# Norm factors kept in PSUM, split weights used for both segments, and two conditions normalised in one VectorE pass

## The chip, the cores and the metric

One core of a Trainium2 chip runs the whole program. The metric is the device time of one execution in microseconds (us). Engines: TensorE (PE in the rows) multiplies matrices and writes to PSUM; VectorE (DVE), ScalarE (ACT) and GpSimd (POOL) do elementwise work; SyncE (SP) issues most DMAs. Each engine runs its own instruction list in order and waits on semaphores for the others.

## The reference, cut to what matters

Two layers of a diffusion trunk run over 640 tokens: 128 context tokens, conditioned by `c_ctx`, and 512 latent tokens, conditioned by `cond`. Layer 0 mixes with a state-space scan and a Conformer convolution, layer 1 with a Fourier transform over grouped channels; a ConvFFN follows each:

```python
for i in range(DEPTH):
    sh1, sc1, gt1, sh2, sc2, gt2 = split(silu(cond) @ w_mod[i] + b_mod[i], 6)
    hm = rmsnorm(x, g_mix[i]) * (1 + sc1) + sh1
    out = mixer(hm)                 # layer 0 ends in "@ w_out", layer 1 in "@ fnet_w + b"
    x = x + gt1 * out
    hf = rmsnorm(x, g_ffn[i]) * (1 + sc2) + sh2
    x = x + gt2 * conv_ffn(hf, w_up, conv_w, w_down)
y = rmsnorm(x, norm_f)
```

So a norm over all 1024 channels stands between each product that ends a sub-layer and the next product. Shift, scale and gate differ between the two conditions.

## The kernel before, in words

Activations lie transposed: 1024 channels are 8 tiles `x[:, k, :]` of 128 partitions by 640 tokens. Every fp32 product is done in three passes, as high part times high part, low times high and high times low (xh·wh, xl·wh, xh·wl; L224 to L233). `weights` (L202) loads a raw weight tile with a DMA from SP; `split` (L210) makes wh by a cast on ScalarE (L218) and wl by a subtraction on GpSimd (L221). Three buffers of each stand in the pool `wp`, five of raw.

For the last part of a product before a norm, the tokens are cut in two segments (`by_segment`, L378): all 8 output tiles m of segment 0, then all 8 of segment 1. Each tile goes through `residual` (L356, VectorE, reading PSUM), a square on ScalarE (L320) and an addition on VectorE (L324). After the eighth tile `finish` (L326) sums over partitions with a matmul by ones (L331, rows named `acc<-ssq,ones` and `acc<-sqt,ones`), and `rstd` (L292) makes the factor `bc`, which is the same on all partitions: one activation (L296) and three VectorE instructions (L297 to L299). The loads and splits of all 8 weight tiles are made once for each segment.

While TensorE works on segment 1, `then` normalises segment 0: `norm_split` (L345) multiplies x by `bc` and the scale A on VectorE (L342, one instruction for each condition), adds the shift on ScalarE (L350, which writes xh) and takes the rest on VectorE (L351, xl). Tile k is emitted NLAG = 4 output tiles late. The next consumer also starts early: `first_up` (L410) holds three w_up tiles, `FIRST`, and multiplies segment 0 of them for k = 0 to 3 before the second `finish` and for k = 4 to 7 after it; `rest` does segment 1 and `mods_between` (L430), the products of the next conditioning vectors (L440, 32 matmul records).

There are four such places, which the text calls A to D:

- A: the last half of `@ w_out`, segments of 320 tokens (607.9 to 661 us); segment 0 holds both conditions (128 and 192 tokens).
- B: the end of the first ConvFFN, going into the Fourier mixer; segments of 384 and 256 tokens.
- C: the end of `@ fnet_w`, like A.
- D: the end of the second ConvFFN, going into the final norm; 384 and 256 tokens.

PSUM is, from A on, four accumulators of 128 x 1024 fp32, which `acc` (L146) takes from one pool in rotation; in A, B and C a `finish` takes one for its sum and frees it after `rstd`. During the scan (250 to 510 us) there are other pools. The order within each engine isn't written by hand: a scheduler chooses it from dependences, pools and its own costs, so it can move lines that the diff doesn't touch.

Of the kernel before, what the change touches and what calls it, by code (L numbers as in the profile page):

```python
# [15 lines left out]
P = 128  # L16
D = 1024
# [31 lines left out]
NLAG = 4  # L49
RAWB = 5  # L50
# [86 lines left out]
def _body(nc, tc, st, A, O, dbg):  # L137
# [8 lines left out]
    def acc():  # L146
        return pools["acc"].tile([P, 1024], F32, tag="acc", name="acc")
# [6 lines left out]
    def set_banks(accs, small):  # L154

        while open_:
            open_.pop().__exit__(None, None, None)
        pools.clear()
        for name, n in (("acc", accs), ("misc", small)):
            if n:  # L160
                open_.append(tc.tile_pool(name=f"{name}{accs}", bufs=n, space=PS))
                pools[name] = open_[-1].__enter__()
# [141 lines left out]
    class SumSq:  # L304
# [3 lines left out]
        def __init__(self, bc=None, apart=True):  # L308
            self.apart = apart
            self.a = sm.tile([P, T], F32, tag="ssq", name="ssq", bufs=1)  # L310
            self.last = {}
            self.bc = bc or sm.tile([P, T], F32, tag="yss", name="bc", bufs=1)
# [13 lines left out]
        def finish(self, s, o):  # L326

            ps = misc()[:, 0:size(s)]
# [3 lines left out]
            bc = self.bc[:, o:o + size(s)]  # L332
            rstd(ps, bc)
            return bc
# [10 lines left out]
    def norm_split(x, bc, a, sh, k, xh, xl, s, gap=0):  # L345
        t = temp("hmt")
        modulated(t, x, bc, a, k, s)
        for sub, o, j in pieces(s):
            to = (sub[0] + j * gap, *sub[1:])
            S.activation(tok(xh[:, k, :], to), tok(t, sub), AF.Identity, bias=sh[:, k, j:j + 1])  # L350
            V.scalar_tensor_tensor(tok(xl[:, k, :], to), in0=tok(t, sub), scalar=sh[:, k, j:j + 1],  # L351
                                   in1=tok(xh[:, k, :], to).bitcast(F32), op0=ADD, op1=SUB)

# [24 lines left out]
    def by_segment(src, k0, acts, x, gt, segs, then, early=None):  # L378


        ss = SumSq()
        bc = {}
        early = early or (lambda k: None)
        for i, s in enumerate(segs):
            def after(m, ps):
                residual(x, m, ps, gt, s)
                ss.add(x[:, m, :], m, s)
                if m == 0:
                    rsqrt_table(x[:, m, s[0]:s[0] + 1])
                if i and m >= NLAG:  # L390
                    then(bc[0], segs[0], m - NLAG)

            product(src, k0, acts, (s,), after)
            if i:
                for k in range(KD - NLAG):
                    early(k)
            bc[i] = ss.finish(s, i * size(segs[0]))
# [3 lines left out]
        for k in range(KD):  # L401
            then(bc[1], segs[1], k)

    def transition(src, k0, acts, x, after, gt, then, early):
# [3 lines left out]
        by_segment(src, k0 + n, acts[n:], x, gt, SEGS, then, early)  # L408
# [664 lines left out]
    def ffn(l, x, xh, xl, background, mods, rest, segs, then, early=None):  # L1073
# [4 lines left out]
        with tc.tile_pool(name=f"ff{l}", bufs=1) as fp:  # L1078
# [62 lines left out]
            by_segment(wdn, *pend, x, gt, segs, then, early)  # L1141
# [215 lines left out]
```

## Time and profile before

| | us |
|---|---|
| runs | 1727.39, 1727.5, 1730.4 (median 1727.5) |
| profiled execution | 1728.85 |
| its span | 1727.1 |
| PE busy | 1636.6 (95%) |
| DVE busy | 1358.5 (79%) |
| ACT busy | 698.2 (40%) |
| POOL busy | 804.9 (47%) |

Times in rows are microseconds from the start of the span. A row of a timeline is start, duration, engine, line, operation, output<-inputs, shape and count; a bracket gives the idle time of that engine just before it and who ended it. Matmul ends are modelled, so the distance between two starts (the pitch) says more than a duration. The granted clock of TensorE is given as a share of 2.4 GHz.

### The profile page before, as it was taken

What the parts mean: (1) busy time and instruction counts of PE and PEld (TensorE: products, weight loads), DVE (VectorE), ACT (ScalarE), POOL (GpSimd) and SP (SyncE); (2) the same over time, 40 slices, a digit from 0 to 9 for tenths busy, and PEclk for the clock granted to TensorE, in tenths of its full rate; (3) what the DMA queues carried; (4) which work ended last, traced back from release to release, by engine and by line L of the source; (5) the groups of instructions that cost most, each with busy time, mean ns of one, the idle gap of its engine ahead of it and who ended that gap; (6) DMA issues with size and microseconds to landing.
All of it is one profiled execution on the core that took longest, in us unless ns stands there. A gap on an engine that the chain in (4) does not pass through costs nothing.

```text
span 1727.1 us, 27861 instructions
## 1 busy us (share of the span) xinstructions
PE 1636.6 (95%) x10794; PEld 1570.9 (91%) x10794; DVE 1358.5 (79%) x2398; ACT 698.2 (40%) x1211; POOL 804.9 (47%) x526
## 2 busy tenths in 40 slices
PE   8898998999899989999999999889899999999997
PEld 5797988889799979999999999779799999999996
DVE  7788696978764788899999999864899848818846
ACT  4322236888853254322331232545633223313324
POOL 1342335655653444563555465404446545534544
PEclk9999999999999999999999999999999999999998
DMA  7455332332332443235224323402532222222123
GB/s 299 155 170 178 120 122 86 111 105 70 96 131 96 136 132 98 62 105 191 71 86 159 134 59 107 144 26 74 176 110 86 75 86 74 73 86 74 47 59 116
DMA packets 81911, 189.20 MB, mean 110 GB/s; under 512 B 7540, under 2 KB 33043, under 8 KB 81780
## 3 DMA queue, kind: packets, MB, share of 16 engines
q1 hardware_dynamic: 78980, 184.29, 33.8%
q10 hardware_dynamic: 2800, 3.15, 0.6%
q8 instruction: 85, 1.39, 0.3%
q14 instruction: 46, 0.38, 0.1%
HBM read 183.57 MB, written 3.83 MB: 109 GB/s over the span
## 4 chain that ended last, share of the span: by engine, by line
PE 43%; DVE 22%; issue 3%; ACT 2%; POOL 1%; DMA 0%; DVEq 0%; POOLq 0%; ACTq 0%
PE acc L229 40%; DVE cva L1104 8%; DVE mm L270 6%; DVE x L356 2%; DVE modc L274 1%; DVE cva L1093 1%; DVE ssq L324 1%; POOL wl L221 1%; PE acc L331 1%; PE acc L440 1%; ACT sqt L320 1%; DVE x L1261 1%; PE acc L1228 0%; DVE hmt L342 0%; ACT fh L1235 0%
## 5 line engine op out<-in xcount | busy, mean ns | idle before, releaser
L221 POOL TENSOR_TENSOR wl<-raw,wh 128x512 fp32r<-128x512 f32 (+5 forms) x314 | 561.6, 1797 | 660.8 <-ACT wh L218 658.2
L229 PE MATMUL acc<-xh,wh 128*128 128x320 f32 (+2 forms) x2064 | 490.1, 315 | 14.8 <-ACT wh L218 7.1
L229 PE MATMUL acc<-xh,wl 128*128 128x320 f32 (+2 forms) x2064 | 487.8, 313 | 6.8 <-POOL wl L221 6.8
L1104 DVE SCALAR_TENSOR_TENSOR cva<-acc,cw,cva 128x504 f32<-128x504 f32 (+2 forms) x704 | 479.2, 692 | 16.6
L229 PE MATMUL acc<-xl,wh 128*128 128x320 f32 (+2 forms) x2064 | 488.2, 313 | 0.2
L218 ACT CAST wh<-raw 128x512 fp32r<-128x512 f32 (+5 forms) x314 | 238.3, 769 | 573.9 <-PE acc L229 413.6
L229 PEld LDWEIGHTS acc<-xh,wh 128*128 128x128 f32 (+1 forms) x2064 | 352.1, 190 | 21.6 <-ACT wh L218 9.1
L229 PEld LDWEIGHTS acc<-xh,wl 128*128 128x128 f32 (+1 forms) x2064 | 351.5, 190 | 9.3 <-POOL wl L221 8.3
L229 PEld LDWEIGHTS acc<-xl,wh 128*128 128x128 f32 (+1 forms) x2064 | 351.9, 190 | 2.6 <-issue 0.9
L356 DVE SCALAR_TENSOR_TENSOR x<-acc,modc,x 128x128 f32<-128x128 f32 (+2 forms) x240 | 112.3, 498 | 126.8 <-PE acc L229 125.8
L229 PE MATMUL acc<-fh,wl 128*128 128x320 f32 (+2 forms) x832 | 206.7, 311 | 2.9 <-POOL wl L221 2.8
L229 PE MATMUL acc<-fh,wh 128*128 128x320 f32 (+2 forms) x832 | 206.6, 311 | 2.2 <-DVE x L356 2.2
L229 PE MATMUL acc<-fl,wh 128*128 128x320 f32 (+2 forms) x832 | 206.4, 310 | 0.0
L229 PEld LDWEIGHTS acc<-fh,wl 128*128 128x128 f32 x832 | 143.8, 189 | 4.6 <-POOL wl L221 4.3
L229 PEld LDWEIGHTS acc<-fh,wh 128*128 128x128 f32 x832 | 143.9, 189 | 2.9 <-issue 2.5
L229 PEld LDWEIGHTS acc<-fl,wh 128*128 128x128 f32 x832 | 143.6, 188 | 0.6
L270 DVE SCALAR_TENSOR_TENSOR mm<-mm 128x1024 f32<-128x1024 f32 x80 | 138.1, 1726 | 1.2 <-DMA mm<-in_w_modT 0.2
L1119 POOL TENSOR_TENSOR cva<-cva 128x640 f32<-128x640 f32 x44 | 72.2, 1641 | 87.8 <-ACT cva L1118 87.8
L270 DVE SCALAR_TENSOR_TENSOR mjunk<-mraw,crow 128x1024 f32<-128x1024 f32 x68 | 97.4, 1433 | 7.8 <-DMA mraw<-in_w_modT 7.4
L1093 DVE SCALAR_TENSOR_TENSOR cva<-acc,cw,cva 128x127 f32<-128x127 f32 x176 | 61.0, 346 | 49.3 <-ACT cva L1089 44.2
L1123 POOL TENSOR_TENSOR fl<-cva,fh 128x640 fp32r<-128x640 f32 x44 | 71.0, 1613 | 34.5 <-ACT fh L1122 34.5
L1118 ACT ACTIVATE cva<-cva 128x640 f32<-128x640 f32 x44 | 32.4, 737 | 119.9 <-DVE cva L1104 113.3
(248 smaller groups left out, 1896.8 us busy)
## 6 DMA issues: line engine op xcount, KB each, us to landing
raw<-in_ffn_w_up SPq DMA_DIRECT2D x88, 512.0 KB, 3.6
raw<-in_w_in SPq DMA_DIRECT2D x40, 512.0 KB, 3.7
mm<-in_w_modT SPq DMA_DIRECT2D x40, 512.0 KB, 3.6
mraw<-in_w_modT SPq DMA_DIRECT2D x34, 512.0 KB, 3.7
e<-acsd SPq DMA_DIRECT2D x40, 256.0 KB, 3.2
raw<-in_ffn_w_down SPq DMA_DIRECT2D x32, 256.0 KB, 2.6
raw<-in_ffn_w_down SPq DMA_DIRECT2D x16, 448.0 KB, 3.4
raw<-in_w_out SPq DMA_DIRECT2D x24, 256.0 KB, 3.2
```

Source lines behind the costliest of these rows:

```text
L218: S.copy(wh[:, ks, :], raw[:, ks, :])
L221: G.tensor_tensor(wl[:, ks, :], raw[:, ks, :], wh[:, ks, :].bitcast(F32), op=SUB)
L229: PE.matmul(part(ps, s), lhsT=wt[:, k, :], rhs=tok(at, s), start=(k == 0 and p == 0), stop=(k == n - 1 and p == 2))
L270: V.scalar_tensor_tensor(junk, in0=raw[:, cs_], scalar=1.0, in1=crow[j][:, cs_], op0=MULT, op1=MULT, accum_out=m[:, 2 * o + j:2 * o + j + 1])
L274: V.tensor_scalar(modc[l][:, i, :], m[:, 0:2], b, None, op0=ADD)
L320: S.activation(t, tok(x_ap, s), AF.Square)
L356: last = V.scalar_tensor_tensor(tok(x[:, m, :], sub), in0=part(ps, s, o, sub), scalar=gt[:, m, j:j + 1], in1=tok(x[:, m, :], sub), op0=MUL ...
L1093: V.scalar_tensor_tensor(a[:, lo:hi], in0=ps[:, BASE + lo + d:BASE + hi + d], scalar=w(1, c), in1=a[:, lo:hi], op0=MULT, op1=ADD)
L1104: last = V.scalar_tensor_tensor(av[:, r0:r1, c0:c1], in0=pv[:, r0 + dr_:r1 + dr_, c0 + dc:c1 + dc], scalar=w(r, c), in1=av[:, r0:r1, c0:c1 ...
L1118: S.activation(cv[1], cv[1], AF.Silu)
L1119: G.tensor_tensor(cv[0], cv[0], cv[1], op=MULT)
L1123: G.tensor_tensor(l_, cv[0], h_.bitcast(F32), op=SUB)
```

## The change

Three edits in the code of `by_segment` and its helpers:

1. `acc` turns explicitly over tags acc0 to acc3. `SumSq(held=True)` takes one accumulator out of that turn at the first `finish`; the sum and the factor `bc` of both segments stay in it (segment 0 from column 0, segment 1 from 512) until `by_segment` ends. `rstd` works in a scratch tile `t` and writes `bc` with its last instruction. This holds in A, B and C; D keeps `bc` in SBUF.
2. Weight tiles split for segment 0 are used again for segment 1. In A and C (`kept=4`) tiles 4 to 7 stay in a pool of their own and 1 to 3 in `wp`, so only tile 0 is loaded and split again, and segment 1 goes in the order 1, 2, 3, 0, 4, 5, 6, 7. In B and D (`kept=0`) the order is 5, 6, 7, 0 to 4 with three tiles used again. That is 20 DMAs, 20 casts and 20 subtractions fewer.
3. `norm_split` for a segment with two conditions (segment 0 of A and C): VectorE multiplies x by `bc` over 320 tokens at once; ScalarE applies scale and shift in place for each condition and copies to xh; VectorE subtracts over 320. Four VectorE and two ScalarE instructions become two and three, for each of 8 tiles.

```diff
+    def acc(hold=False):
+        i = turn["next"]
+        if i == turn["held"]:
+            i = (i + 1) % turn["n"]
+        turn["next"] = (i + 1) % turn["n"]
+        if hold:
+            turn["held"] = i
+        return pools["acc"].tile([P, 1024], F32, tag=f"acc{i}", name="acc", bufs=1)
...
-        y = sm.tile([P, 384], F32, tag="sqt", name="ry", bufs=3)[:, 0:n]
+        y, t = (sm.tile([P, 384], F32, tag="sqt", name="ry", bufs=3)[:, 0:n] for _ in range(2))
         S.activation(y, ps, AF.Abs_reciprocal_sqrt, scale=1.0 / D, bias=eps)
-        V.tensor_tensor(out, y, y, op=MULT)
-        V.scalar_tensor_tensor(out, in0=ps, scalar=D * EPS, in1=out, op0=ADD, op1=MULT)
-        V.scalar_tensor_tensor(out, in0=out, scalar=-3.0 * D, in1=y, op0=ADD, op1=MULT)
+        V.tensor_tensor(t, y, y, op=MULT)
+        V.scalar_tensor_tensor(t, in0=ps, scalar=D * EPS, in1=t, op0=ADD, op1=MULT)
+        V.scalar_tensor_tensor(out, in0=t, scalar=-3.0 * D, in1=y, op0=ADD, op1=MULT)
...
+            if self.held:
+                if self.bc is None:
+                    self.bc = acc(True)
+                ps = bc = self.bc[:, 512 * (o > 0):512 * (o > 0) + size(s)]
...
+            V.tensor_tensor(tok(t, s), tok(x[:, k, :], s), flat(bc, s), op=MULT)
+            for sub, _, j in ps:
+                S.activation(tok(t, sub), tok(t, sub), AF.Identity, scale=a[:, k, j:j + 1], bias=sh[:, k, j:j + 1])
+            S.copy(tok(xh[:, k, :], s), tok(t, s))
+            V.tensor_tensor(tok(xl[:, k, :], s), tok(t, s), tok(xh[:, k, :], s).bitcast(F32), op=SUB)
...
+        n = KD - kept
+        there = list(range(n - 3, n))
+        orders = (range(KD), there + list(range(n - 3)) + list(range(n, KD)))
...
+                for p, m in enumerate(orders[i]):
+                    ps = acc()
+                    mtile(ps, weight(i, m), acts, (s,))
+                    residual(x, m, ps, gt, s)
+                    ss.add(x[:, m, :], p, s)
+                    if i and p >= NLAG:
+                        then(bc[0], segs[0], p - NLAG)
...
-        by_segment(src, k0 + n, acts[n:], x, gt, SEGS, then, early)
+        by_segment(src, k0 + n, acts[n:], x, gt, SEGS, then, early, kept=KEPT)
...
-            by_segment(wdn, *pend, x, gt, segs, then, early)
+            by_segment(wdn, *pend, x, gt, segs, then, early, held=segs is RUNS)
```

The scheduler's order moves with it. First VectorE at the end of segment 1 in A. Before, the list is the following; L342 and L351 are the norm of segment 0, tiles up to k = 7, and L297 begins the second `rstd`.

```order
L342 SCALAR_TENSOR_TENSOR hmt<-x,A_91,bc 128x128
L342 SCALAR_TENSOR_TENSOR hmt<-x,A_91,bc 128x192
L351 SCALAR_TENSOR_TENSOR xl<-hmt,modc_88,xh 128x192
L351 SCALAR_TENSOR_TENSOR xl<-hmt,modc_88,xh 128x128
L351 SCALAR_TENSOR_TENSOR xl<-hmt,modc_88,xh 128x192
L297 TENSOR_TENSOR bc<-ry 128x320
```

After the change, VectorE has at that place (L379 and L383 are the multiplication and the subtraction of the new norm, L310 the last instruction of `rstd`, L359 the norm of segment 1):

```order
L309 SCALAR_TENSOR_TENSOR ry<-acc,ry 128x320
L310 SCALAR_TENSOR_TENSOR acc<-ry 128x320
L379 TENSOR_TENSOR hmt<-x,acc 128x320 x2
L383 TENSOR_TENSOR xl<-hmt,xh 128x320
L379 TENSOR_TENSOR hmt<-x,acc 128x320
L383 TENSOR_TENSOR xl<-hmt,xh 128x320
L379 TENSOR_TENSOR hmt<-x,acc 128x320
L383 TENSOR_TENSOR xl<-hmt,xh 128x320
L359 SCALAR_TENSOR_TENSOR hmt<-x,A_91,acc 128x320
```

The norm of segment 0 for k = 4 to 7 now stands behind the second `rstd`; it stood ahead of it. C has the same order, and in B the same tiles follow the second `rstd`.

Then TensorE in A, behind the early products of the three `FIRST` tiles. Before (L440 is the conditioning product, L229 a product of `FIRST`, segment 1):

```order
L229 MATMUL acc<-xh,wl 128x320
L440 MATMUL acc<-mraw,sc__86 2x128 x16
L229 MATMUL acc<-xh,wh 128x320
L229 MATMUL acc<-xl,wh 128x320
L229 MATMUL acc<-xh,wl 128x320
```

After (L492 is the conditioning product; the rows with x2 are both segments of the next whole w_up tile):

```order
L240 MATMUL acc<-xh,wl 128x320
L240 MATMUL acc<-xh,wh 128x320 x2
L240 MATMUL acc<-xl,wh 128x320 x2
...
L240 MATMUL acc<-xh,wl 128x320 x2
L492 MATMUL acc<-mraw,sc__86 2x128 x16
L240 MATMUL acc<-xh,wh 128x320 x2
```

The conditioning product moved behind the rest of `FIRST` and behind one whole further w_up tile. In C it moves the same way.

The third place is ScalarE in the scan, of which no line is changed. Before (L296 is `rstd`'s activation; ACT_TABLE_LOAD loads the table of functions for the next activation):

```order
L296 ACT_TABLE_LOAD
L296 ACTIVATE ry<-misc,eps 128x320 x2
L844 ACT_TABLE_LOAD
L844 ACTIVATE e<-e 128x512
L747 ACT_TABLE_LOAD
```

After (L307 is `rstd`'s activation, L896 is L844 of before, L799 is L747 of before):

```order
L307 ACT_TABLE_LOAD
L307 ACTIVATE ry<-misc,eps 128x320
L896 ACT_TABLE_LOAD
L896 ACTIVATE e<-e 128x512
L799 ACT_TABLE_LOAD
L799 ACTIVATE cvb<-cvb 128x642
L307 ACT_TABLE_LOAD
L307 ACTIVATE ry<-misc,eps 128x320
```

The two activations of the LayerNorm's `rstd`, which now needs a second scratch tile, are apart. From there on the order of all engines differs through the rest of the scan; over the whole program ScalarE has 50 table loads where it had 46.

## Rows read from the trace of the kernel before

**Rows 1.** Page, section 1: busy time, share of the span, instructions of each engine.
```profile
PE 1636.6 (95%) x10794; PEld 1570.9 (91%) x10794; DVE 1358.5 (79%) x2398; ACT 698.2 (40%) x1211; POOL 804.9 (47%) x526
```

**Rows 2.** Stretches: length, busy PE, PEld, DVE, ACT, POOL, granted clock, DMA share, GB/s.
```profile
607.90:661.00 53.10, 45.99 (x283) 42.10 (x284) 44.46 (x84) 25.53 (x51) 20.63 (x12) 0.94 0.41 127
633.00:637.00 4.00, 4.00 (x16) 4.00 (x17) 3.96 (x6) 0.98 (x3) 2.12 (x1) 0.50 0.56 169
1211.30:1264.70 53.40, 45.92 (x282) 42.12 (x283) 44.20 (x83) 31.16 (x56) 20.57 (x12) 0.94 0.51 166
1097.20:1150.00 52.80, 41.77 (x258) 35.27 (x257) 40.74 (x111) 25.28 (x57) 12.47 (x15) 0.90 0.34 105
250.00:510.00 260.00, 237.09 (x1527) 222.07 (x1527) 198.04 (x372) 200.95 (x417) 149.81 (x147) 0.97 0.31 92
```

**Rows 3.** Timeline of PE in A.
```profile
608.79 0.78 PE L331 MATMUL acc<-ssq,ones 128*128 128x320 f32 x2 [0.95 <-DVE ssq L324]
...
630.35 0.63 PE L229 MATMUL acc<-xh,wh 128*128 128x320 f32 x1 [2.33 <-ACT wh L218]
632.80 0.64 PE L229 MATMUL acc<-xh,wl 128*128 128x320 f32 x1 [1.55 <-POOL wl L221]
...
635.63 0.47 PE L229 MATMUL acc<-xh,wh 128*128 128x320 f32 x1
635.90 0.47 PE L229 MATMUL acc<-xl,wh 128*128 128x320 f32 x1
...
643.09 0.30 PE L229 MATMUL acc<-xh,wh 128*128 128x320 f32 x1
643.24 0.31 PE L229 MATMUL acc<-xl,wh 128*128 128x320 f32 x1
...
645.82 3.66 PE L440 MATMUL acc<-mraw,sc__86 128*2 128x128 f32 x32
```

**Rows 4.** Chain of waits in A: start, duration, what.
```profile
624.92 2.64 POOL wl L221
627.55 2.79 issue
...
630.38 2.38 POOL wl L221
...
632.80 6.73 PE acc L229 x31
```

**Rows 5.** Timeline of DVE in A.
```profile
612.83 1.30 DVE L299 SCALAR_TENSOR_TENSOR bc<-bc,ry 128x320 f32<-128x320 f32 x1
...
625.25 2.45 DVE L342 SCALAR_TENSOR_TENSOR hmt<-x,A,bc 128x128 f32<-128x128 f32 x1
627.62 0.54 DVE L356 SCALAR_TENSOR_TENSOR x<-acc,modc,x 128x320 f32<-128x320 f32 x1
...
629.41 0.54 DVE L356 SCALAR_TENSOR_TENSOR x<-acc,modc,x 128x320 f32<-128x320 f32 x1
629.87 0.66 DVE L351 SCALAR_TENSOR_TENSOR xl<-hmt,modc,xh 128x128 fp32r<-128x128 f32 x2
...
641.21 0.49 DVE L297 TENSOR_TENSOR bc<-ry 128x320 f32<-128x320 f32 x1 [1.26 <-ACT ry L296]
```

**Rows 6.** All instructions by line and shape: count, busy time, mean ns, idle before.
```profile
L356 DVE SCALAR_TENSOR_TENSOR x<-acc,modc,x 128x320 f32<-128x320 f32 x16 | 8.6, 539 | 0.0
L350 ACT ACTIVATE xh<-hmt,modc 128x320 fp32r<-128x320 f32 x16 | 8.3, 559 | 8.5 <-DVE hmt L342 8.5
L342 DVE SCALAR_TENSOR_TENSOR hmt<-x,A,bc 128x320 f32<-128x320 f32 x16 | 8.1, 546 | 0.1
```

**Rows 7.** Timeline of ACT in C, before the second norm factor.
```profile
1241.73 1.28 ACT L454 ACT_TABLE_LOAD   x1
1243.02 1.06 ACT L454 ACTIVATE mm<-mm 128x1024 f32<-128x1024 f32 x1
```

**Rows 8.** Timeline of PE in B, the longest wait there.
```profile
1140.17 0.58 PE L1228 MATMUL acc<-dfts,v 128*128 128x128 f32 x1 [5.84 <-ACT v L1216]
```

More of the change, by code (lines that the diff above doesn't have):

```diff
@@ L49 @@
 NLAG = 4
+KEPT = 4
 RAWB = 5
@@ L144, in _body @@
     V, S, G, PE = nc.vector, nc.scalar, nc.gpsimd, nc.tensor
-    def acc():
-        return pools["acc"].tile([P, 1024], F32, tag="acc", name="acc")
+    turn = {"n": 0, "next": 0, "held": None}
+    def acc(hold=False):
[6 more added lines that the diff above has]
+        return pools["acc"].tile([P, 1024], F32, tag=f"acc{i}", name="acc", bufs=1)
     def misc():
@@ L158, in set_banks @@
         pools.clear()
+        turn.update(n=accs, next=0, held=None)
         for name, n in (("acc", accs), ("misc", small)):
             if n:
-                open_.append(tc.tile_pool(name=f"{name}{accs}", bufs=n, space=PS))
+                open_.append(tc.tile_pool(name=f"{name}{accs}", bufs=n if name == "misc" else 1, space=PS))
                 pools[name] = open_[-1].__enter__()
@@ L304, in _body, with __init__ @@
     class SumSq:
-        def __init__(self, bc=None, apart=True):
+        def __init__(self, bc=None, apart=True, held=False):
             self.apart = apart
+            self.held = held
             self.a = sm.tile([P, T], F32, tag="ssq", name="ssq", bufs=1)
             self.last = {}
-            self.bc = bc or sm.tile([P, T], F32, tag="yss", name="bc", bufs=1)
+            self.bc = None if held else bc or sm.tile([P, T], F32, tag="yss", name="bc", bufs=1)
         def add(self, x_ap, k, s):
@@ L326, in finish @@
         def finish(self, s, o):
[L328 removed]
+            if self.held:
+                if self.bc is None:
+                    self.bc = acc(True)
+                ps = bc = self.bc[:, 512 * (o > 0):512 * (o > 0) + size(s)]
+            else:
+                ps = misc()[:, 0:size(s)]
+                bc = self.bc[:, o:o + size(s)]
             parts = [tok(self.a, s)] + ([self.last[s]] if self.apart else [])
@@ L346, in norm_split @@
         t = temp("hmt")
-        modulated(t, x, bc, a, k, s)
-        for sub, o, j in pieces(s):
-            to = (sub[0] + j * gap, *sub[1:])
+        ps = [(sub, (sub[0] + j * gap, *sub[1:]), j) for sub, _, j in pieces(s)]
+        if len(ps) == 1:
+            (sub, to, j), = ps
+            modulated(t, x, bc, a, k, s)
             S.activation(tok(xh[:, k, :], to), tok(t, sub), AF.Identity, bias=sh[:, k, j:j + 1])
@@ L376, in ffn_norm, with by_segment, weight @@
         return xh, xl, then
-    def by_segment(src, k0, acts, x, gt, segs, then, early=None):
-        ss = SumSq()
+    def by_segment(src, k0, acts, x, gt, segs, then, early=None, kept=0, held=True):
+        ss = SumSq(held=held)
         bc = {}
         early = early or (lambda k: None)
[L384 to L397, printed above, removed]
+        n = KD - kept
+        there = list(range(n - 3, n))
+        orders = (range(KD), there + list(range(n - 3)) + list(range(n, KD)))
+        with tc.tile_pool(name="kp", bufs=1) as kp:
+            ws = {}
+            def weight(i, m):
+                if i and m in ws:
+                    return ws[m]
+                if m < n:
+                    w = weights(src, m, k0, len(acts))
+                else:
+                    raw = wp.tile([P, len(acts), P], F32, tag="raw", name="raw", bufs=RAWB)
+                    nc.sync.dma_start(raw, src[m][:, k0:k0 + len(acts), :])
+                    w = split(raw, kp, (f"kh{m}", f"kl{m}"), 1)
+                if m >= n - 3:
+                    ws[m] = w
+                return w
+            for i, s in enumerate(segs):
+                for p, m in enumerate(orders[i]):
[3 more added lines that the diff above has]
+                    ss.add(x[:, m, :], p, s)
+                    if p == 0:
+                        rsqrt_table(x[:, m, s[0]:s[0] + 1])
+                    if i and p >= NLAG:
+                        then(bc[0], segs[0], p - NLAG)
+                if i:
+                    for k in range(KD - NLAG):
+                        early(k)
+                bc[i] = ss.finish(s, i * size(segs[0]))
         for k in range(KD - NLAG, KD):
@@ L402, in by_segment @@
             then(bc[1], segs[1], k)
+        turn["held"] = None
     def transition(src, k0, acts, x, after, gt, then, early):
```

8 lines of the change are left out of this document (7 added, 1 removed).

## The prediction

> **What bounds the kernel now.** I read the page first: TensorE is busy for 95% of the span, VectorE for 79%, ScalarE for 40%, GpSimd for 47% [rows 1]. So an engine beside TensorE counts only where TensorE waits for it. The table of stretches shows where that may be. TensorE idles for 7.1 us of A's 53.1, 7.5 of C's 53.4, 11.0 of B's 52.8 and 22.9 of the scan's 260 [rows 2].
>
> The timeline of TensorE says how much of A is loss. At full clock a product of 320 tokens starts 0.147 us after the last (643.09 to 643.24) [rows 3]. A holds 96 such products for segment 1, 72 early ones and 72 of the rest: 240 x 0.147 = 35.3. Two sums by ones take about 1.1 each (2.2), the conditioning products 3.66 and their transposes some 0.5 [rows 3]. That is 41.7, so 11.4 of the 53.1 us are lost: waits, and a stretch at half clock. The waits stand close together: 2.33 us for wh at 630.35, 1.55 for wl at 632.80, and three more of 0.4 to 1.1 for wl before them. From 632.8 to 637 the granted clock is 0.50, the lower level of 1.2 GHz, and the pitch 0.27 (635.63 to 635.90), after TensorE had those waits [rows 2, 3]. C shows the same five waits within 0.4 us of A's; with the same work its loss is 53.4 - 41.7 = 11.7.
>
> The chain of waits names who is late: subtractions on GpSimd (2.64 us, then 2.38) with 2.79 us of issue between them, in which a cast waits its turn on ScalarE [rows 4]. ScalarE waits for squares, squares for residuals, and residuals stand behind a VectorE instruction that takes 2.45 us for 128 elements; the residual of 320 behind it takes 0.54 [rows 5]. The subtraction at 624.92 ends 0.1 us before that long instruction does [rows 4, 5]. So the loss is a knot of VectorE and GpSimd holding each other up. Here the Trainium skill fits, in "SBUF — State Buffer", section "SBUF: two separate sides": a VectorE instruction with two SBUF inputs and a GpSimd one that reads SBUF use one shared port pair, locked by whichever starts first. By that rule a multiplication with `bc` in PSUM would not be held, but a subtraction xl with both inputs in SBUF still would; nothing below is computed from it.
>
> **What it removes.** In A and C seven of eight splits of the second segment go, each a cast, a GpSimd subtraction and a DMA. But three of TensorE's five waits, the two longest among them, are not for w_out: the last three splits of that stretch (2.64 and twice about 2.4 us [rows 4]) are the three w_up tiles of `FIRST`, and they stay. They can come earlier, as GpSimd has only tile 0 ahead of them. VectorE loses 16 instructions in each place.
>
> **A after the change, step by step.** The first factor was done at 612.83 + 1.30 = 614.1 [rows 5]; 0.8 of that was a stall beside a split, and that split goes: 613.3. Until the residual of the last tile VectorE then has seven residuals, six additions of squares, four multiplications and four subtractions of the norm, 21 instructions of 320 elements. Two of them start 0.46 apart (629.41 to 629.87) [rows 5]. The new multiplication reads `bc` from PSUM, which no row of before shows at this shape for a norm; the nearest are the residual, which reads PSUM, with a mean of 539 ns, and L342 with both tensors in SBUF, with 546 [rows 6]. I take no difference; from -0.1 to +0.2 us each, 16 in A and C before the waits end, moves the sum by -1.6 to +3.2. So 21 x 0.46 = 9.7, and VectorE is there at 623.0 if nothing holds it. Four GpSimd subtractions remain beside it (tile 0 and three w_up). At worst each costs VectorE what the long row did, 2.45 - 0.34 = 2.1, so 0 to 8.4; I take half, 4.2: 627.2.
>
> TensorE begins segment 1 at about 608.8 [rows 3] and needs 1.1 + 96 x 0.147 = 15.2: 624.0. One accumulator is held, so the third tile of `FIRST` takes the bank of the last output tile and must wait for its residual. Six early products (0.9) go before it. Wait one: 627.2 - 624.9 = 2.3 us.
>
> Wait two is new. Before, VectorE's list had the norm of segment 0 complete ahead of the second `rstd`, and TensorE went on with k = 4 to 7 without a gap while `rstd` began at 641.21 [rows 5]. Now tiles 4 to 7 stand behind it. After TensorE's sum by ones come ScalarE's activation (about 0.55), three VectorE instructions (about 0.5 each, as L297 [rows 5]), the multiplication (0.5), and on ScalarE two scalings and a copy; the copy is like L350 of 320 elements, 0.56 mean [rows 6], the pair shorter each: 1.2. Together 3.75 us in which TensorE has nothing: its next instruction is k = 4.
>
> With the 0.95 at 608.79 [rows 3] A has waits of 0.95 + 2.3 + 3.75 = 7.0 where it lost 11.4: gain 4.4. At best VectorE isn't held (wait one at 0) and ScalarE starts the second activation, and each step behind it, without delay (wait two some 2.7): 8. At worst VectorE is held for the full 8.4 (4.2 more) and the clock halves for some 16 products (2 us, as in [rows 2]): -1.8. Behind wait two early(4) to early(7) and the rest follow at VectorE's pace: it needs about 1 us a tile, TensorE 9 x 0.147 = 1.3.
>
> The conditioning products move behind a further w_up tile, since their turn of the accumulators is the first `FIRST` bank, which the convolution must read first. 48 products (7 us) stand ahead of them as cover; the convolution of the bank begins on VectorE beside these. I cost it at nothing; if the cover is short, up to 3 us in each of A and C.
>
> **C** is A with one difference. Two background activations (1.06 each) and their table load (1.28) [rows 7] stood on either side of the second `ry`; now both, with table loads before and behind, stand ahead of it: 2 x 1.06 + 2 x 1.28 = 4.7 us on ScalarE, some of it before the sum is ready. I charge 1 us: gain 3.4 to 3.7, take 3.5, bounds -2 to 8.
>
> **B** loses three splits of eight and has the same late tiles. Its longest wait, 5.84 us for v, lies behind both norms [rows 8] and stays. +0.5, from -1.5 to 2. **D** keeps `bc` in SBUF; the five splits which remain take the last places, so the end is set as before: +0.3, 0 to 1.
>
> **The scan** computes the same with another order of all engines. The four extra table loads cost 4 x 1.28 = 5.1 us on ScalarE, busy there for 201 of 260 us [rows 2, 7]. How much reaches TensorE no row tells: with 22.9 us idle there, a better order could return a few and a worse one add more. Taken: -1.5, from -6 to 4.
>
> **Sum.** 4.4 + 3.5 + 0.5 + 0.3 - 1.5 = 7.2 us. The profiled execution took 1728.85, 1.75 above its span; 1728.85 - 7.2 = 1721.6. The median of the runs is 1.35 below that execution, so in their measure 1720.3.
>
> **Rivals.**
> *Full gain.* If the splits alone cause the knot, VectorE isn't held and wait one goes; if the activation of the second sum also finds an idle ScalarE, wait two is some 2.7. Then A loses 3.7 of 11.4, gain 7.7, C 8, and the scan costs nothing: 16.5 with B and D, time 1711. For it: all five waits name a split [rows 3, 4]. Against: the last three splits stay, and the order shows the new wait.
> *The wait moves.* VectorE is held for most of 8.4 us by the w_up splits, wait two is followed by half clock as after 630.35, and the conditioning products wait: A and C give some 1 us together, and the time is 1726.5 with the scan as it is. For it: the three 1024-element splits did the worst damage before. A page of the Trainium skill speaks the same way: "VectorE: DVE Perf Modes", section "Specifications", has VectorE closer to SBUF and ScalarE to PSUM, so factors read from PSUM should cost VectorE more. The 539 beside 546 ns [rows 6] shows no such surcharge; with it the time would lie toward this rival.
> *Slower, by the scan.* Table loads and squares in the middle of a head's chain (the LayerNorm's second `ry` now behind an exponential and a Silu) hold `e` and `w`, for which GpSimd and TensorE wait. Each load of 1.28 that stands in such a chain delays all behind it. If the scan loses 13 us, the rest gains 8.7, and the time is 1732. It decides from a loss of about 9 us, where TensorE's idle time in the scan passes 32.
> *The change doesn't do what it says:* no; the lists show 20 subtractions fewer, so I give this nothing.
>
> **How the numbers follow.** Forecast 0.45, full gain 0.17, the wait moves 0.22, slower by the scan 0.16. A measurement can tell about 0.2%, 3.5 us, from no change: faster means below 1724, slower above 1731. The forecast's own range, from A's and C's middle bounds, is 1715 to 1726; nine tenths of it is below 1724 (0.40). With the full gain and a tenth of the second rival, faster is 0.60; same is the rest of the forecast and of the second, and the lighter half of the scan's cases, 0.26; slower 0.14. The range that leaves out two tenths is 1711 to 1730.
>
> **What would show it.** Right: in A five waits for wl or wh shrink to one at tile 0 at most; a wait of 3 to 4 us before the first product of k = 4, ended by ScalarE or VectorE; A of 48 to 50 us; one long VectorE instruction beside each w_up split and none beside segment 1's earlier tiles. Wrong: no idle time after the second sum by ones; multiplications L379 well above 0.55 us without a split beside them; a scan whose idle time differs by more than 6 us from 22.9; a wait of the conditioning products.

## The result, and the profile after

The changed kernel takes 1753.55 us (median of 4 runs, 1750.24 to 1754.81), the kernel before 1728.58: the ratio is 1.0141, 95% interval 1.0123 to 1.0158. It is 25 us slower where a gain of 7 us was forecast. The profiled execution took 1750.24 us with a span of 1748.4, 21.3 longer than that of before.

The page's busy times hold what the change set out to do: VectorE is busy 20.7 us less and GpSimd 29 us less than in [rows 1]. TensorE isn't faster; its busy time has grown by 7.6 us with the same number of instructions, and the mean granted clock of the profiled execution is 0.978 where it was 0.981.

```profile
PE 1644.2 (94%) x10794; PEld 1575.2 (90%) x10794; DVE 1337.8 (77%) x2366; ACT 700.0 (40%) x1211; POOL 775.9 (44%) x506
```

To find where the time went, the same instructions were looked up in both timelines: the first CB product of the scan (`cvc,cvb`), the eleventh of the 16 VectorE instructions that scale its output `yT` (L965 before, L1017 after; "the scan's end"), the two sums by ones of A and C, a ScalarE cast `fh` well behind the second of them ("past": the fifth behind A, the ninth behind C), and in B a product `d,f` of the Fourier mixer. Lengths in us:

| stretch | before | after | difference |
|---|---|---|---|
| start to the scan's first CB product | 271.6 | 271.0 | -0.6 |
| scan | 256.8 | 265.6 | +8.8 |
| scan's end to A's first sum | 80.3 | 85.2 | +4.9 |
| A: first sum to second sum | 30.6 | 27.0 | -3.6 |
| A: second sum to past | 83.0 | 90.5 | +7.5 |
| to B's first sum | 375.7 | 375.4 | -0.3 |
| B: first sum to past | 32.6 | 36.8 | +4.2 |
| to C's first sum | 81.4 | 78.8 | -2.6 |
| C: first sum to second sum | 31.0 | 27.0 | -4.0 |
| C: second sum to past | 182.2 | 190.3 | +8.1 |
| to the end of the span, with D | 301.8 | 300.8 | -1.0 |

The splits did give time, 3.6 and 4.0 us between the sums. Behind the second sum twice as much is lost, and the scan and the way to A lose the rest.

TensorE's timeline in A answers to [rows 3]. The waits for wl and wh are gone; three are for residuals on VectorE, and one stands where there was none, ahead of the first product of k = 4:

```profile
635.99 0.42 PE L240 MATMUL acc<-yh,wh 128*128 128x320 f32 x1 [0.72 <-DVE x L387]
641.28 0.38 PE L240 MATMUL acc<-xh,wh 128*128 128x320 f32 x1 [2.74 <-DVE x L387]
642.77 0.39 PE L240 MATMUL acc<-xh,wh 128*128 128x320 f32 x1 [0.82 <-DVE x L387]
...
648.81 0.70 PE L349 MATMUL acc<-ssq,ones 128*128 128x320 f32 x2
649.35 0.70 PE L349 MATMUL acc<-sqt,ones 128*128 128x320 f32 x2
654.47 0.63 PE L240 MATMUL acc<-xh,wh 128*128 128x320 f32 x1 [4.42 <-ACT xh L382]
...
655.69 0.47 PE L240 MATMUL acc<-xh,wh 128*128 128x320 f32 x1
655.96 0.47 PE L240 MATMUL acc<-xl,wh 128*128 128x320 f32 x1
```

The stretch behind that wait (columns as in [rows 2]) runs at a granted clock of 0.50, 1.2 GHz, for 22 products; at 0.267 instead of 0.147 us each that is 2.6 us more. Wait and clock make 7.1 of the 7.5 us. The second row below is the stretch behind the three waits for residuals.

```profile
654.40:660.50 6.10, 6.03 (x22) 5.79 (x23) 4.98 (x11) 4.79 (x12) 0.00 (x0) 0.50 0.01 3
642.00:647.00 5.00, 4.23 (x18) 4.26 (x19) 0.63 (x2) 0.47 (x1) 0.00 (x0) 0.66 0.33 130
```

C has a wait of 4.80 at the same place, and in B a wait of 3.27 stands where the kernel before had none:

```profile
1263.35 0.63 PE L240 MATMUL acc<-xh,wh 128*128 128x320 f32 x1 [4.80 <-ACT xh L382]
```

```profile
1141.02 0.48 PE L1229 MATMUL acc<-d,f 128*128 128x256 f32 x1 [3.27 <-ACT f L1214]
```

The chain of waits of the changed kernel shows each step of A's wait (start, duration, what). TensorE's second sum, ScalarE's activation, three instructions of `rstd`, the multiplication, and the way over ScalarE follow one another with nothing beside them:

```profile
648.97 1.09 PE acc L349 x4
...
650.09 0.54 ACT ry L307
...
650.65 0.50 DVE ry L308
...
651.18 0.50 DVE ry L309
...
651.70 0.51 DVE acc L310
...
652.24 0.50 DVE hmt L379
...
652.76 1.31 ACT hmt L381 x3
654.07 0.36 ACT xh L382
```

The longest VectorE instructions of A between the sums are additions beside splits, and the multiplications with PSUM (L379) are never among them:

```profile
628.58 1.72 DVE L336 TENSOR_TENSOR ssq<-ssq,sqt 128x320 f32<-128x320 f32 x1 [0.20 <-ACT sqt L332]
...
633.04 2.43 DVE L336 TENSOR_TENSOR ssq<-ssq,sqt 128x320 f32<-128x320 f32 x1 [0.40 <-ACT sqt L332]
...
638.52 2.15 DVE L336 TENSOR_TENSOR ssq<-ssq,sqt 128x320 f32<-128x320 f32 x1 [0.41 <-ACT sqt L332]
```

GpSimd's subtractions in that stretch, the first of them for tile 0, and the VectorE instruction beside that one, the last of the first `rstd`:

```profile
625.35 1.30 POOL L232 TENSOR_TENSOR wl<-raw,wh 128x512 fp32r<-128x512 f32 x1 [12.89 <-ACT wh L229]
...
627.54 2.41 POOL L232 TENSOR_TENSOR wl<-raw,wh 128x1024 fp32r<-128x1024 f32 x1 [0.89 <-ACT wh L229]
632.72 2.40 POOL L232 TENSOR_TENSOR wl<-raw,wh 128x1024 fp32r<-128x1024 f32 x1 [2.77 <-ACT wh L229]
637.81 2.52 POOL L232 TENSOR_TENSOR wl<-raw,wh 128x1024 fp32r<-128x1024 f32 x1 [2.69 <-ACT wh L229]
```

```profile
625.83 1.17 DVE L310 SCALAR_TENSOR_TENSOR acc<-ry 128x320 f32<-128x320 f32 x1
```

Ahead of A's first sum TensorE waits where it did not before, and ScalarE's casts wait for DMAs:

```profile
607.14 0.41 PE L240 MATMUL acc<-yh,wh 128*128 128x320 f32 x1 [1.81 <-ACT wh L229]
609.76 0.63 PE L240 MATMUL acc<-yh,wl 128*128 128x320 f32 x1 [2.07 <-POOL wl L232]
```

```profile
599.65 1.14 ACT L229 CAST wh<-raw 128x512 fp32r<-128x512 f32 x2 [4.47 <-DMA raw<-in_w_out]
605.28 2.85 ACT L229 CAST wh<-raw 128x512 fp32r<-128x512 f32 x5 [4.48 <-DMA raw<-in_w_out]
```

### The profile page after: what moved, and what is told of

It is laid out like the page before. It is cut to its first block, busy times and chain, and to the rows that moved or that the text cites. A ratio compares the mean times of both kernels' runs of the same rounds, so it can differ in the third digit from the quotient of the medians.

```text
span 1748.4 us, 27700 instructions
## 1 busy us (share of the span) xinstructions
PE 1644.2 (94%) x10794; PEld 1575.2 (90%) x10794; DVE 1337.8 (77%) x2366; ACT 700.0 (40%) x1211; POOL 775.9 (44%) x506
## 3 DMA queue, kind: packets, MB, share of 16 engines
q10 hardware_dynamic: 2800, 3.15, 0.6%
## 4 chain that ended last, share of the span: by engine, by line
PE 53%; DVE 32%; ACT 5%; issue 4%; POOL 3%; DMA 2%; ACTq 0%; DVEq 0%; SPq 0%; POOLq 0%
PE acc L240 48%; DVE cva L1156 9%; DVE mm L281 7%; DVE mjunk L281 2%; DVE x L387 2%; DVE modc L285 2%; DVE ssq L336 2%; DVE cva L1145 1%; POOL wl L232 1%; PE misc L738 1%; POOL xdd L843 1%; DMA raw<-in_w_in 1%; ACT wh L229 1%; ACT sqt L332 1%; PE acc L349 1%
## 5 line engine op out<-in xcount | busy, mean ns | idle before, releaser
L232 POOL TENSOR_TENSOR wl<-raw,wh 128x512 fp32r<-128x512 f32 (+5 forms) x294 | 532.0, 1820 | 700.4 <-ACT wh L229 693.4
L1156 DVE SCALAR_TENSOR_TENSOR cva<-acc,cw,cva 128x441 f32<-128x441 f32 (+2 forms) x704 | 480.7, 692 | 17.1
L229 ACT CAST wh<-raw 128x512 fp32r<-128x512 f32 (+5 forms) x294 | 225.3, 779 | 577.8 <-PE acc L240 421.6
L1170 ACT ACTIVATE cva<-cva 128x640 f32<-128x640 f32 x44 | 32.4, 736 | 117.4 <-DVE cva L1156 117.3
```

What stands on the lines that cost most here:

```text
L229: S.copy(wh[:, ks, :], raw[:, ks, :])
L232: G.tensor_tensor(wl[:, ks, :], raw[:, ks, :], wh[:, ks, :].bitcast(F32), op=SUB)
L1156: last = V.scalar_tensor_tensor(av[:, r0:r1, c0:c1], in0=pv[:, r0 + dr_:r1 + dr_, c0 + dc:c1 + dc], scalar=w(r, c), in1=av[:, r0:r1, c0:c1 ...
L1170: S.activation(cv[1], cv[1], AF.Silu)
```

## The experiments

Theory O: the work is cheaper, and the order in which the scheduler then writes it costs more than that. Rival P: the new work itself is dear (PSUM reads, ScalarE's longer way, one accumulator fewer). "Old rotation" means accumulators from one pool, as before; with it and the factor in SBUF the scan has the order of the kernel before on every engine. Times are medians; every interval is the ratio to runs of before on the same chip.

**e1_scan**: all three edits undone, explicit turn and scratch tile left.

```diff
-KEPT = 4
+KEPT = 0
-        orders = (range(KD), there + list(range(n - 3)) + list(range(n, KD)))
+        orders = (range(KD), range(KD))
-                if m >= n - 3:
+                if False:
-        elif gap:
+        elif True:
-    def by_segment(..., kept=0, held=True):
+    def by_segment(..., kept=0, held=False):
```

> All three edits are undone at A to D (no held accumulator, no weights used twice, the old norm of four VectorE instructions); what stays is the explicit turn of the accumulators and the scratch tile of rstd, with which the scheduler writes the scan in the order of the changed kernel. Theory O (the loss comes from the order: 8 us in the scan, and at A and C the second norm factor ahead of the norm of tiles 4 to 7): the scan loses its 8 us here and A to D are as before, 1735 to 1739 against 1728.6. Rival P (the loss comes from the work itself: factors read from PSUM, the norm's longer way over ScalarE, one accumulator fewer): the scan loses because of what the held accumulator and the kept weights do to it, so nothing is lost here, 1727 to 1730.

1744.89 us, ratio 1.0097 (1.0080 to 1.0114). The scan takes 265.7 us, 8.9 more than before. That was O's part. But A and C lost too, 5.3 and 6.3 us behind the second sum, which nobody expected: the conditioning products stand behind a further w_up tile, whose weights aren't split yet (in A, waits of 1.03 for wh and 1.59 for wl at 664.9 and 667.3, then half clock from 667.8 for 3.4 us). Turn and scratch tile, with none of the edits, cost 17 us, and the time lies above the bands of both theories.

**e2_norm_first**: the changed kernel, norm of tiles 4 to 7 emitted ahead of the second sum.

```diff
                 if i:
                     for k in range(KD - NLAG):
                         early(k)
+                    for k in range(KD - NLAG, KD):
+                        then(bc[0], segs[0], k)
                 bc[i] = ss.finish(s, i * size(segs[0]))
         for k in range(KD - NLAG, KD):
-            then(bc[0], segs[0], k)
             early(k)
```

> The changed kernel, with the norm of segment 0 for tiles 4 to 7 emitted ahead of the second sum by ones in the code, so that on VectorE it stands ahead of the second rstd again, as before the change; the scan keeps the changed order. Theory O: the wait of 4.4 us before the first product of k = 4 and the half clock behind it (some 2.7 us) go in A and in C, 14 us together, 1738 to 1742 where the changed kernel takes 1753.6. Rival P: the norm by way of ScalarE in place is late wherever it stands, the wait shrinks to 2 to 3 us and the half clock stays, 1747 to 1752.

1732.56 us, 1.0024 (1.0015 to 1.0034): 21 us less than the changed kernel by this order alone; the conditioning products stay where the change had put them, 156 products of w_up tiles behind the second sum. Behind the second sum A takes 83.0 us and C 183.4, B 32.4 in all; before had 83.0, 182.2 and 32.6. The gain is above O's figure because B gives 4.4 back too. No wait stands behind the second sum of A. The norm's way over ScalarE and PSUM is the same work here, so P falls for these stretches. What is left against before is the scan (265.7) and the way to A (85.3).

**e3_no_held**: edits 2 and 3 without edit 1, old rotation.

```diff
-    def by_segment(..., kept=0, held=True):
+    def by_segment(..., kept=0, held=False):
     def acc(hold=False):
+        return pools["acc"].tile([P, 1024], F32, tag="acc", name="acc")
```

and `rstd` with one scratch tile where the factor is in SBUF, as in the next two.

> Edits 2 and 3 without edit 1: weights used for both segments and the norm of two conditions in one pass, the factor in SBUF, accumulators in the old rotation; the scan has the order of the kernel before, and the norm of tiles 4 to 7 stands ahead of the second rstd. Theory O: the gain that was forecast for the splits comes out, 4 to 6 us in each of A and C and nothing lost in the scan, 1717 to 1722. Rival P: the norm's way over ScalarE costs what the splits give, 1727 to 1732.

1725.18 us, 0.9986 (0.9976 to 0.9995). A small gain, less than O expected: the scan is as before (255.6), but the way to A takes 86.4.

**e4_reuse**: edit 2 alone, that is e3 with the old norm.

```diff
-        elif gap:
+        elif True:
```

> Edit 2 alone: weights used for both segments, old norm, factor in SBUF, old rotation, the scan in the order of before. Theory O: fewer splits free VectorE and GpSimd, but VectorE keeps its 16 extra instructions in each place, so somewhat less than edits 2 and 3 together: 1719 to 1725. Rival P: edit 2 gives the whole gain and edit 3 takes part of it back, so this one is faster than edits 2 and 3 together by 3 us or more, 1716 to 1721.

1723.43 us, 0.9972 (0.9961 to 0.9984). The time lies in O's band, though edit 2 alone isn't slower than edits 2 and 3 together, as O had it. From sum to sum A and C take 25.8 us each, 4.8 and 5.2 less than before: the splits were worth that. The way to A again takes 86.0. Casts wait there for a DMA as in the changed kernel (4.48 and 4.01 us at 591.15 and 596.30), though the DMAs of these tiles are issued at most 0.5 us later than before. ScalarE's list explains it: kept tiles have buffers of their own, free early, and the scheduler put the casts of tiles 4 to 7 between those of tiles 0 to 3.

**e5_casts_in_order**: e4 with that order mended.

```diff
-            S.copy(wh[:, ks, :], raw[:, ks, :])
+            turn["cast"] = S.copy(wh[:, ks, :], raw[:, ks, :])
...
-                    w = split(raw, kp, (f"kh{m}", f"kl{m}"), 1)
+                    with tc.issue_after(turn["cast"].ins):
+                        w = split(raw, kp, (f"kh{m}", f"kl{m}"), 1)
```

> Edit 2 alone, as in the run before it, and one line more: the cast of a kept tile is queued on ScalarE behind the cast of the tile before it. Without that line the scheduler puts casts of kept tiles, whose buffers are free early, ahead of the casts of tiles 1 to 3, and ScalarE's list then stands still until the kept tile's DMA has landed: TensorE waited 1.6 and 1.8 us for wh and wl at the start of segment 0 of A, and A's segment 0 began 3.7 us late. Theory H (that order is the cause): these waits go and the whole run is 3 to 4 us faster than edit 2 alone, 1719 to 1721. Rival D (the DMAs themselves land later because of the kept tiles): the waits stay, 1722 to 1724.

1721.06 us, 0.9970 (0.9957 to 0.9983). The way to A takes 80.7 us, the waits there are gone, and ScalarE's casts wait for TensorE instead:

```profile
591.09 0.62 ACT L231 CAST wh<-raw 128x512 fp32r<-128x512 f32 x1 [2.90 <-PE acc L242]
593.00 1.14 ACT L231 CAST wh<-raw 128x512 fp32r<-128x512 f32 x2 [1.29 <-PE acc L242]
```

H holds for these waits, and not for the whole time: the ratio to before is within 0.0002 of that of e4 (0.9972). The 5.3 us gained on the way to A come back as 1.5 and 1.6 between the sums of A and C, where TensorE meets VectorE's residuals (waits of 2.25, 0.87 and 1.21 us in A), and as 1.8 between B and C. That the casts in order also shorten a whole run is seen with the new norm, in e10 against e3 (0.9961, 0.9986) and e11 against e7 (0.9979, 1.0013).

**e6_scratch**: the kernel before, `rstd` with a second scratch tile.

```diff
-        y = sm.tile([P, 384], F32, tag="sqt", name="ry", bufs=3)[:, 0:n]
+        y, t = (sm.tile([P, 384], F32, tag="sqt", name="ry", bufs=3)[:, 0:n] for _ in range(2))
```

with `t` for `out` in the two instructions behind it.

> The kernel before with one thing changed: rstd computes in a second tile of the tag sqt, as in the changed kernel. Accumulators, weights and norms are as before; A to D have the order of before, and the scan's order changes in its second half only, with 52 loads of a function table on ScalarE in the program instead of 46. Theory L (the extra loads and the later LayerNorm factor are what the scan lost): a part of the 8 us, 3 to 8, so 1731 to 1736. Rival R (the explicit turn's reordering cost it, from the first half of the scan on): within 1 us of before, 1727 to 1729.

1731.95 us, 1.0030 (1.0017 to 1.0042): the scan takes 261.9, 5.1 more than before.

**e7_norm_first_one_scratch**: e2 without that tile in the scan.

```diff
+        t = sm.tile([P, 384], F32, tag="sqt", name="ry", bufs=3)[:, 0:n] if held else out
```

> The changed kernel with the norm of tiles 4 to 7 ahead of the second sum (1732.6 us), and rstd with the second scratch tile only where the factor is held in PSUM, so that the LayerNorm in the scan has it as before; the scan then has the explicit turn's order without the scratch's, 46 loads of a table instead of 52. Theory L: the scan's loss goes in good part, 1725 to 1729. Rival R: it stays, 1731 to 1734.

1728.70 us, 1.0013 (1.0003 to 1.0022). The scan takes 259.9, 3.1 over before. So the scratch tile alone costs 5 us there and the turn's order alone 3, together 8.2 of the 8.8 that were lost. Kernels with the same order of the scan differ by up to 2.2 us in it. The stretches of the scan in before, changed kernel, e6 and e7 (columns as in [rows 2]):

```profile
271.60:528.50 256.90, 235.22 (x1511) 221.66 (x1510) 199.29 (x379) 201.12 (x417) 147.51 (x143) 0.97 0.32 95
```

```profile
271.00:536.60 265.60, 239.77 (x1510) 224.05 (x1510) 196.85 (x379) 206.43 (x421) 145.31 (x142) 0.96 0.30 92
```

```profile
270.10:531.90 261.80, 237.61 (x1510) 222.34 (x1509) 201.23 (x378) 208.58 (x423) 146.71 (x143) 0.97 0.31 93
```

```profile
271.40:531.40 260.00, 237.84 (x1510) 224.30 (x1510) 195.16 (x379) 198.64 (x415) 146.66 (x142) 0.96 0.31 94
```

In the changed kernel TensorE's idle time grew by 4.1 us (25.8 against 21.7) and its busy time by 4.6 at the same work, with a granted clock of 0.96 against 0.97. ScalarE has 36 table loads there instead of 32 in the changed kernel, 38 in e6 and 30 in e7, so loads alone don't explain it: e7 has fewer than before and is slower than it.

**e8_norm_alone**: edit 3 on the kernel before.

> Edit 3 alone on the kernel before: two conditions multiplied and subtracted at once on VectorE, scale and shift on ScalarE; weights loaded and split twice, factor in SBUF, old rotation, the scan as before. Theory O, as it stands after the first four runs (edits 2 and 3 together were 1.7 us slower than edit 2 alone): 16 VectorE instructions fewer give nothing, since the waits are for splits, and ScalarE's longer way delays casts a little: 1728 to 1731. Rival V: VectorE was part of the knot, so fewer instructions there free the splits, 1724 to 1726.

1726.19 us, 0.9997 (0.9988 to 1.0006): no change that can be told, below the expected band of O and above V's. Its edit is the last branch of `norm_split` in the diff of the change, alone.

**e9_held_alone**: edit 1 alone, that is e1 with `held=True`.

> Edit 1 alone, with the explicit turn and the scratch tile that come with it: the factor in a held accumulator, all 16 weight tiles of A and C split twice, old norm. VectorE's list has the second rstd ahead of tiles 4 to 7 in A, B and C, as in the changed kernel. Theory O: the scan loses its 8 us, the three places some 7, 4 and 7, and in A and C the next w_up tile isn't ready as in the first run (5 each, unless the wait before it covers that): 1752 to 1762. Rival J (the order flips only where the splits are gone, or costs nothing with the slower splits): 1742 to 1748, like the first run.

1751.80 us, 1.0129 (1.0113 to 1.0145), 0.2 us below O's band. Edit 1 with its turn and scratch tile makes nearly the whole loss: scan 267.8, behind the second sum 89.3 in A and 188.1 in C, B 37.5. The wait before k = 4 is 3.40 us in A here, with the old norm, and 4.42 in the changed kernel: once the order is turned, the longer way over ScalarE adds 1.0, and rival P has that part.

**e10_reuse_norm_casts**: e3 with e5's two lines.

> Edits 2 and 3 with the casts of kept tiles in order, factor in SBUF, old rotation. Without the splits TensorE in A waited for residuals on VectorE (2.3, 0.9 and 1.2 us in edit 2 alone with casts in order), and edit 3 takes 16 instructions from VectorE there. Theory V: these waits shrink and the run is 1 to 4 us faster than edit 2 with casts in order, 1717 to 1720. Rival O2 (ScalarE's longer way makes xh late instead, as in edits 2 and 3 without ordered casts, where TensorE waited 3.2 us for xh): 1721 to 1724.

1721.89 us, 0.9961 (0.9946 to 0.9976). With e5 it is the fastest, and beats both kernels; the two can't be told apart by these intervals. O2 was right about the wait: TensorE stands 3.15 us for xh.

```profile
628.44 0.61 PE L242 MATMUL acc<-xh,wh 128*128 128x320 f32 x1 [3.15 <-ACT xh L385]
```

**e11_all_reordered**: the changed kernel with the edits of e2, e5 and e7 together.

> The changed kernel with all three edits and three orders mended: the norm of tiles 4 to 7 ahead of the second sum, rstd with one scratch tile outside the held factor, casts of kept tiles in order. Against the run with the first two of these (1728.7 us) it lacks only the 4 to 5 us before the first sum of A. Theory H: 1723 to 1726, faster than before by a little, since 3 us of the explicit turn's order in the scan stay. Rival D: 1727 to 1730.

1724.62 us, 0.9979 (0.9969 to 0.9989). H holds. All three edits are in it, and it is 29 us faster than the changed kernel; only the order and a scratch tile differ.

**e12_flip_alone**: the kernel before, norm of tiles 4 to 7 queued on VectorE behind the second `rstd`.

```diff
         for k in range(KD - NLAG, KD):
-            then(bc[0], segs[0], k)
+            with tc.issue_after(ss.done.ins):
+                then(bc[0], segs[0], k)
             early(k)
```

> The kernel before with one order changed: the norm of segment 0 for tiles 4 to 7 is queued on VectorE behind the last instruction of the second rstd, in A, B and C; nothing else of the change, the scan as before. Theory O (this order alone is the price): a wait of 3 to 4.5 us before the first product of k = 4 in A and C and half clock behind it, some 5 to 7 us each, and 2 to 4 in B: 1739 to 1746. Rival M (the wait is the price of the longer ScalarE way of edit 3 or of the held accumulator, and the order by itself is hidden by the late splits): 1728 to 1733.

1736.18 us, 1.0044 (1.0027 to 1.0060), between the theories. B loses 6.1 (its new wait is 3.23 us here), but A and C only 2.4 and 2.2, and the reason stands in the timeline: the scheduler moved half of the conditioning products (L441) into the gap. The edit acts in D too, though the expectation names only A, B and C: from D's second sum to the end takes 13.6 us where it took 11.2. The changed kernel does not have that loss (10.6).

```profile
643.02 1.69 PE L441 MATMUL acc<-mraw,sc__86 128*2 128x128 f32 x14 [1.67 <-DVE bc L298]
```

So my theory lacked a part, and three more runs made a square on e10: order of the norm, place of the conditioning products.

**e13_flip**, e10 with e12's edit:

> Edits 2 and 3 with casts in order and the old rotation (1721.9 us), with one order changed: the norm of tiles 4 to 7 behind the second rstd on VectorE in A, B and C. The conditioning products then stand, by the scheduler, right behind the second sum. Theory T (order and conditioning products together make the loss): they fill most of the wait, 0 to 3 us lost in each of A and C and 4 to 6 in B, 1727 to 1733. Rival A (the order alone, dearer with early splits): 7 to 8 in A and C, 4 to 6 in B, 1739 to 1743.

**e14_flip_mods_behind**, e13 and

```diff
-            mods_between(MODSB[2 * l])
             for b, w in zip(FIRST, ws):
                 mtile(ps0[b], w, acts, SEGS[1:])
+            with tc.issue_after(turn["mm"].ins):
+                mods_between(MODSB[2 * l])
```

(`turn["mm"]` is the last matmul of the rest; the conditioning products then stand 108 products of w_up tiles behind the second sum, and in the changed kernel 156):

> The same with the conditioning products queued behind the rest of the first w_up tiles, as the changed kernel has them. Theory T: the wait is open, some 4 us, with half clock behind it, so 6 to 8 us lost in each of A and C against edits 2 and 3 with casts in order, and 4 to 6 in B: 1738 to 1744. Rival A: as the run without this move within 2 us.

**e15_mods_behind**, the same move without the flip:

> Edits 2 and 3 with casts in order, the norm of tiles 4 to 7 ahead of the second rstd, and only the conditioning products moved behind the rest of the first w_up tiles. Theory T: with the norm in time nothing needs cover, and the next w_up tile's weights are split early enough: within 2 us of 1721.9. Rival W (as in the first run, the next w_up tile comes too early for its weights): 5 us in each of A and C, 1730 to 1733.

| us behind the second sum | e10 | e13 | e14 | e15 |
|---|---|---|---|---|
| A | 83.0 | 86.1 | 91.6 | 84.4 |
| C | 182.6 | 186.2 | 191.5 | 183.6 |
| B, whole | 31.5 | 38.7 | 37.7 | 32.6 |
| median of the run | 1721.89 | 1737.15 | 1742.71 | 1727.52 |

The ratios are 1.0065 (1.0046 to 1.0084), 1.0107 (1.0082 to 1.0133) and 1.0003 (0.9991 to 1.0014). In A the order costs 3.1, the move 1.4, both 8.6; in C 3.6, 1.0 and 8.9. The joint figure is about what the changed kernel lost (7.5 and 8.1). e14's wait shows why (first row); in e13 conditioning products start 1.67 us after the sum and fill it (second row). The move costs e15 its 1.4 and 1.0 in three short waits behind these products (0.45, 0.31 and 0.50 us in A). At the changed kernel's place it costs nothing in A when the norm is in time: e2 takes 83.0 there.

```profile
638.85 0.63 PE L242 MATMUL acc<-xh,wh 128*128 128x320 f32 x1 [4.29 <-ACT xh L385]
```

```profile
637.80 2.78 PE L498 MATMUL acc<-mraw,sc__86 128*2 128x128 f32 x24 [1.67 <-DVE bc L312]
```

T holds for A and C in kind, its losses up to 0.9 us above its bands, and e14's time lies in T's band, 5.6 us above e13's, against rival A. As whole times e13 came out above T's band, by B (7.2 against 4 to 6), by D (2.9 to the end of the span) and by 2.6 us between C's sums; e15 is 3.6 us above its band, so by the whole time the move isn't free.

Between C's sums e13 and e15 take 29.3 and 29.6 us, e10 and e14 26.7 and 26.4. The waits there are alike (1.9, 1.1, and 2.7 or 3.15 us in all four), but the granted clock is 0.83 in the first two and 0.94 in the others; no run shows why.

Of the profiled executions e15's is also 3.2 us later than e10's ahead of A, where the code is equal: the start to the scan differs by up to 4.5 us from execution to execution of these kernels (269.7 to 274.2), so single traces were compared by stretches and not by their ends. The whole times alone do not show that order and move cost more together than apart (0.9961 for e10, 1.0065 and 1.0003 for each, 1.0107 for both); the stretches of A and C do.

## Why the prediction was wrong

- **The order of A's wait two was read rightly, its price was not.** The prediction had a wait of 3.75 us before k = 4; it is 4.42, and 4.80 in C. 0.5 of the difference is the way over ScalarE, 1.7 us in the chain where 1.2 was taken. The step that failed is the overlap and the clock behind the wait. The sum set waits of 7.0 against a loss of 11.4 us that held half clock too, and put half clock of the new stretch only into the worst case. TensorE had idled for just 7.1 us in A [rows 2], so by the prediction's own figures the waits gave 0.1 us, and nearly all of the gain of 4.4 was half clock, taken as gone without a reason. Measured: waits of 0.72, 2.74, 0.82 and 4.42 make 8.7 where 7.0 was forecast, and 22 products at 1.2 GHz behind the last of them cost 2.6. A was to gain 4.4 from sum to past; it lost 3.9 (-3.6 and +7.5). C, to gain 3.5, lost 4.1; the background activations, for which 1 us was charged, show in a wait 0.4 longer than A's.
- **"The conditioning products ... I cost at nothing" failed.** They were asked whether they would wait; they didn't, and with the norm in time their move costs A nothing (e2). What failed is that they were the work that could fill wait two, as e12 shows and e13 to e15 measure: 8.6 us instead of 3.1 in A.
- **B at +0.5 failed in sign.** The same late tiles were named and given no price: 4.2 us lost with a new wait of 3.27, and 6.1 in e12 for the order alone.
- **"Four GpSimd subtractions remain" was right between the sums**, where VectorE is held three times by 1.2 to 2 us (the rows on L336; 0.49 us is its length undisturbed) and once by 0.7 (L310 at 625.83 takes 1.17 us beside the split of tile 0, and 0.51 behind the second sum; the prediction had that stall go with its split). That is 5.5 us in all, inside the bounds of 0 to 8.4 and near the 4.2 taken. The new multiplication takes 0.483 us, less than the 0.54 to 0.55 of the rows it was compared with. Here the Trainium skill's rule in "SBUF — State Buffer", section "SBUF: two separate sides", agrees: each long instruction has two SBUF inputs and lies beside a subtraction. L379, which reads PSUM, has no long one in 16 (mean 483 ns), but only two of the 16 lie beside a subtraction (both 475 ns), so that half of the rule rests on two instructions here.
- **The way to A was missing.** The prediction looked at edit 2 in the second segment alone. In the first its own buffers let casts run ahead of their turn, and ScalarE's list stood: 4.9 us, which go with the casts in order (80.6 in e11 against 85.3 in e7).
- **The scan was taken at -1.5 with a bound of -6; it lost 8.8.** The third rival named this place, and the size at which it decides (9 us) was near; its gains elsewhere did not come, so the time is far beyond it. Its sign, idle time past 32 us, did not show: half of the loss is idle time (4.1 us), and the other half is busy time at a lower clock (4.6), for which the prediction had no term.
- Rival two had the surcharge for reading PSUM, after the Trainium skill's "VectorE: DVE Perf Modes", section "Specifications". No run shows one: L379 with PSUM takes 483 ns on average, L383, a subtraction of the same shape with SBUF alone, 484.

What stays open: which instruction of the reordered scan costs its 3 to 5 us, why the clock there is lower, and whether a mended turn of the accumulators would keep the scan as it was; none of these was tried. e8 leaves open whether edit 3 gains anything by itself.

## What to carry to other kernels

Where a scheduler decides the order, a change to buffers is a change of order everywhere they bear on: look in the lists for what stands ahead of a late wait, and for what could have filled it. A buffer that is free early lets its producer run ahead of its turn, and an in-order engine then waits there with all that is behind it (two waits of 4.5 us for a DMA here). Price a new wait of TensorE with the products behind it at the lower clock, here 2.6 us behind 4.4, and count a loss at the lower clock as gone only where the waits ahead of it go.

## What was not expected of the hardware

After 4.42 us without work TensorE ran 22 products of 320 tokens at 1.2 GHz and was back at 2.4 at 660.6. Behind the three waits of 0.72, 2.74 and 0.82, with products between them, the granted clock was 0.50 as well, from 643.6 to 647.0 (0.66 over 642 to 647). The scan of the changed kernel lost as much to busy time at a lower clock (4.6 us) as to idle time (4.1).
